# One pool for the output stage and the feed-forward weights of a hybrid decoder layer

## The chip, the cores and the metric

The kernel runs on one core of a Trainium2 chip. The metric is the device time of one execution in microseconds (us). TensorE (PE) multiplies matrices and loads their weights in a separate step (PEld), VectorE (DVE) and ScalarE (ACT) do elementwise work and conversions, GpSimd (POOL) does elementwise work on on-chip memory, and SyncE (SP) issues the transfers. Each engine takes its instructions in the order of its own queue.

## The reference

The reference computes one decoder layer on 1024 tokens of width 1024, with 16 learned tokens in front.

```python
u = rmsnorm(h, attn_norm_w[l])
proj = u @ w_in[l]
...
o_gdn = gated_deltanet_group(...)            # 4 heads of 128, chunked delta rule
o_fox = forgetting_attention_group(...)      # 8 heads of 64, softmax with a forget-gate bias
h = h + jnp.concatenate([o_gdn, o_fox], axis=-1) @ w_out[l]
h = h + swiglu(rmsnorm(h, ffn_norm_w[l]), w_gate[l], w_up[l], w_down[l])
...
h = rmsnorm(h, final_norm_w)
return h[:, N_META:]

def swiglu(x, w_gate, w_up, w_down):
    return (jax.nn.silu(x @ w_gate) * (x @ w_up)) @ w_down
```

The feed-forward width is 2816. All values are float32.

## The kernel before

Every float32 product is made of three matmuls on rounded halves: an operand is split into hi (a cast on ACT) and lo (a subtraction on DVE), and hi*hi, hi*lo and lo*hi are summed. The function split does one such split, load_w loads raw weights and splits them into a tile pair of the pool wsp, wout_block does so for one 512-column half of w_out.

The stages up to the attention are not touched. In the attention TensorE runs by an order that a planner (PeOrder, od) writes out; w_out's product with the delta-rule heads (wout_gdn, one unit per column half nb and row tile tt of 128 tokens, twelve matmuls of 512 columns) fills its gaps. There are 16 units, and the last RES = 6 are left over for the time after the attention.

Then comes the output stage. Row tiles are taken in ORDER = (0, 4, 1, 5, 2, 6, 3, 7). For each:

- prep_load loads the attention's result and its normalisers into a tile `of` (POOL adds two halves, L1101; ACT copies 1/sum, L1102).
- prep_pe transposes the normalisers on TensorE (rbt, L1111), multiplies on DVE (L1112) and splits the result into oh and ol (L160, L161).
- load_h fetches the residual (tile hst).
- out_fox(tt, nb) adds w_out's product with the attention heads for one column half: twelve matmuls (wof, L191 to L193), an add on DVE (L1176), and after the second half norm2: the square on ACT (L1044), the power on POOL (L207), the scaling xn on DVE (L1046).
- u_blocks transposes xn (u2t, L1192) and makes the operands of the feed-forward stage on DVE, ACT and POOL (L1197 to L1218).

The feed-forward stage multiplies 2 x 2 blocks with seven instead of eight products, p1 to p7 (a Strassen-Winograd scheme). For each of NF = 11 passes j and each of gate and up (m = "g", "u") w_ops loads two raw tiles, builds sums of their blocks on DVE, and splits each of the seven operands when its turn in ORD comes. block3 does twelve matmuls for one product (L1264), ffn_evict takes it out of the accumulator, down_sums prepares w_down's blocks on POOL (L1274 to L1277). The units of a pass run p1, p6, p2, p7, p5, p4, p3, each for gate and up; in the first pass p1 and p2 are prepared early and run first.

TensorE's order is the program's order in these stages (manual_schedule). The other engines' and SP's order comes from a scheduler that goes by its own time estimates; issue_after only holds an instruction behind another on the same queue. A tile's first write waits until the tile that had the place before it is done with; a pool opened with reuse_waits="tile" waits for the overlapping tiles alone, any other pool for all that lay there. In the kernel before, the first-pass tiles are placed like this:

```python
woc.close()
wrc.close()
f1[0] = f1c.enter_context(tc.tile_pool(name="f1", bufs=1, side="right", reuse_waits="tile"))
```

So the output stage's pool (wo1) and the weight pools (wraw, wsp) end, and the feed-forward weights get a new pool f1 in their place.

Of the kernel before, what the change touches and what calls it, by code (L numbers as in the profile page):

```python
# [95 lines left out]
def tile_hymba_layer(ctx, tc, x, meta, attn_norm_w, w_in, conv_w, a_log, dt_bias, gdn_norm_w,  # L96
# [57 lines left out]
    wraw = wrc.enter_context(tc.tile_pool(name="wraw", bufs=2, side="right"))  # L154
    wsp = wrc.enter_context(tc.tile_pool(name="wsp", bufs=4, side="right"))
# [8 lines left out]
    def load_w(parts, name):  # L164
# [9 lines left out]
        hi = wsp.tile([P, WMAX], F32R, tag="whi", name=f"whi_{name}")  # L174
        lo = wsp.tile([P, WMAX], F32R, tag="wlo", name=f"wlo_{name}")
# [879 lines left out]
    def wout_block(k0, nb):  # L1055
        ws = ([], [])
        for i in range(2):
            hl = load_w([(wout_w(k0 + 2 * i, nb), 1024)], f"wo{k0}_{nb}{i}")
# [23 lines left out]
    od.fill = wout_gdn_all(tiles[:len(tiles) - RES])  # L1082
# [7 lines left out]
    wo2 = woc.enter_context(tc.tile_pool(name="wo1", bufs=1, side="right", reuse_waits="tile"))  # L1090
    turn, ofs, pre_u = {}, {}, {}
# [14 lines left out]
    def prep_pe(tt):  # L1106
        of = ofs[tt]
        oh, ol = (wo_tile(t, [P, 4, P], 2, tt, F32R) for t in ("oh", "ol"))
# [13 lines left out]
    for tag in ("of_0", "of_1", "oh_0", "ol_0", "oh_1", "ol_1", "hst_0", "xn2_0", "hst_1", "xn2_1"):  # L1122
        big = tag[:2] in ("hs", "xn")
        wo2.tile([P, D] if big else [P, 8 if tag[1] == "f" else 4, P], F32R if tag[1] in "hl" else F32, tag=tag,
                 name=f"lay_{tag}")
    nwb2 = wo2.tile([P, D], F32, name="nwb2")
    od.fill = wout_gdn_all(tiles[len(tiles) - RES:])
    prep_load(ORDER[0])
    with tc.issue_after(last_o[0].ins):
        nc.sync.dma_start(nwb2, ffn_norm_w[0].partition_broadcast(P))  # L1130
    prep_load(ORDER[1])
# [7 lines left out]
    peo.close()  # L1139
    rot[0] = 1  # L1140
    wo0c.close()
    alc.close()
    ogc.close()
    akc.close()
    gplc.close()
    H, NF = 512, NFF // 2
    ORD = ("p1", "p6", "p2", "p7", "p5", "p4", "p3")
    CH = ((0, 4), (4, 4), (8, 3))

    def chunked(nm, ps):  # L1150
        t = {(p, f0): dram.tile([P, n, H], F32, name=f"{nm}_{p}{f0}") for p in ps for f0, n in CH}
        return t, {(p, f0 + i): t[p, f0][:, i] for p in ps for f0, n in CH for i in range(n)}

    ao_c, ao_d = chunked("ao", ORD)
    wt_c, wt_d = chunked("wt", ("p5", "p6", "p7", "p4"))
    w_g_v = w_gate.rearrange("(k p) n -> p k n", p=P)
    w_u_v = w_up.rearrange("(k p) n -> p k n", p=P)

    uoc, pfc, f1c = ExitStack(), ExitStack(), ExitStack()
    uop = uoc.enter_context(tc.tile_pool(name="uop", bufs=1, reuse_waits="tile"))  # L1160
    uop.tile([P, 120], F32, name="upad")

    def blk(c, p, nm=None):
        return uop.tile([P, 4, H], F32R, tag=f"u{c}_{p}", name=nm or f"u{c}_{p}")

    uo = {p: tuple(blk(c, p) for c in "hl") for p in ORD}
    pfp = pfc.enter_context(tc.tile_pool(name="pf", bufs=1, reuse_waits="tile"))
# [14 lines left out]

    tops = {}

    def u_blocks(tt):
# [14 lines left out]
        if tt < 4:  # L1200
            br = [wo_tile(f"br{g}", [P, 4, P], 1, tt) for g in range(2)]
# [5 lines left out]
        b12, t2, t3 = (wo_tile(f"ub{i}", [P, 4, P], 1, tt) for i in range(3))  # L1207
# [12 lines left out]
    f1, raw_dma = [None], {}  # L1220
# [7 lines left out]
    def pf_tile(i, nm, dt=F32R):  # L1228
        return pfp.tile([P, D], F32R, tag=f"pf{i}", name=nm)
# [3 lines left out]

    def w_ops(v, j, m):
        r0, r1 = (f1[0].tile([P, D], F32, tag="raw", bufs=4, name=f"raw_{m}{j}_{i}") for i in range(2))
        for r, f in ((r0, j), (r1, j + NF)):
            raw_dma[m, j] = w_raw(r, v, f)
        a11, a12, a21, a22 = r0[:, :H], r0[:, H:], r1[:, :H], r1[:, H:]
        s2, s3, s4 = (f1[0].tile([P, H], F32, tag=f"ws{i}", bufs=2, name=f"ws{i}_{m}{j}") for i in range(3))
        if not j:  # L1240
            V.tensor_tensor(s3, a21, a22, op=ALU.add)
# [3 lines left out]
            V.tensor_tensor(s4, a12, s2, op=ALU.subtract)  # L1245
            V.tensor_tensor(a11, a11, a21, op=ALU.subtract)
            srcs = (None, s2, None, a11, s3, a22, s4)
        else:
            V.tensor_tensor(s3, a11, a21, op=ALU.subtract)
            V.tensor_tensor(a21, a21, a22, op=ALU.add)  # L1250
            V.tensor_tensor(s2, a21, a11, op=ALU.subtract)
            V.tensor_tensor(s4, a12, s2, op=ALU.subtract)
# [294 lines left out]
```

## Time and profile before

| | |
|---|---|
| median of 3 runs | 1349.8 us (1348.13 to 1351.02) |
| profiled execution | 1348.91 us, span of its profile 1347.2 us |
| DVE, ACT, POOL busy in the span | 894.9, 553.9, 426.1 us |
| output stage in the trace | from 612 us (last value product of the attention) to about 727 us |
| feed-forward, first two weight matrices | about 700 to 1129 us |
| w_down and final norm | about 1129 us to the end |

Times in views of the trace count from the start of the span. Busy time of an engine is the time in which it executed something; a wait is put down to the instruction that released it. Weight loads (PEld) overlap with matmuls. "clock" is the share of full speed that was granted to TensorE.

### The profile page before, as it was taken

The page shows a single profiled execution, that of the slowest core. Times are in us where ns is not written, and L with a number is a line of the kernel's source. Part 1 is how long each engine was busy: PE and PEld are TensorE (multiplying, and loading weights), DVE is VectorE, ACT ScalarE, POOL GpSimd, SP SyncE. Part 2 cuts the span into 40 slices and gives each one's busy share as a digit, 9 for nine tenths or more (in the row PEclk, how much of TensorE's full clock was granted, in tenths as well). Part 3 has the DMA queues.
Part 4 walks back from the last instruction along what each step waited for, and adds up shares of the span by engine and source line. Part 5 has one row for each costly group of instructions (what it writes and reads, how often), then busy time and mean ns, then how long its engine had stood idle before and what let it go on. Part 6 is the DMA issues. An engine that isn't in the chain of part 4 may idle for free.

```text
span 1347.2 us, 20241 instructions
## 1 busy us (share of the span) xinstructions
PE 1305.9 (97%) x7442; PEld 1137.6 (84%) x7442; DVE 894.9 (66%) x1509; ACT 553.9 (41%) x926; POOL 426.1 (32%) x414
## 2 busy tenths in 40 slices
PE   8999999999999999999898999999999999999997
PEld 7999998899999877887676888888888888888886
DVE  6465778758446578894879667766777765455644
ACT  6443444322223476883553233333332343333332
POOL 3111114211012255661333545543444343010301
PEclk9999999999999999999988999999999999999999
DMA  8121555684589698846556554454444446954523
GB/s 292 54 84 55 146 163 157 182 236 132 164 267 301 168 286 223 222 115 199 175 154 192 180 177 136 156 168 161 163 158 164 156 176 232 410 205 173 208 71 125
DMA packets 196922, 242.12 MB, mean 180 GB/s; under 512 B 19024, under 2 KB 146888, under 8 KB 193112
## 3 DMA queue, kind: packets, MB, share of 16 engines
q1 hardware_dynamic: 196824, 240.84, 56.4%
q8 instruction: 58, 0.95, 0.3%
q14 instruction: 40, 0.33, 0.1%
HBM read 161.62 MB, written 79.18 MB: 179 GB/s over the span
## 4 chain that ended last, share of the span: by engine, by line
PE 79%; DMA 8%; DVE 7%; issue 2%; SPq 2%; POOL 1%; ACT 1%; POOLq 0%; DVEq 0%; ACTq 0%
PE xp L1433 9%; PE yp L1433 7%; PE ub L1264 5%; PE gd L1264 4%; PE ud L1264 4%; PE ga L1264 4%; PE ua L1264 4%; PE gb L1264 4%; PE pj_fk L201 3%; PE pj_fq L201 3%; PE ue L1264 2%; PE ge L1264 2%; PE pt L967 2%; PE po L988 1%; DMA of<-o_d 1%
## 5 line engine op out<-in xcount | busy, mean ns | idle before, releaser
L161 DVE TENSOR_TENSOR al_p<-ra_p,ah_p 128x2048 fp32r<-128x2048 f32 (+1 forms) x21 | 47.1, 2243 | 92.7 <-ACT ah_p L160 92.7
L920 POOL TENSOR_TENSOR bi<-ccol,cr 128x144 f32<-128x144 f32 (+7 forms) x60 | 69.7, 1167 | 54.5 <-DVE sm L936 32.3
L160 ACT CAST ah_p<-ra_p 128x2048 fp32r<-128x2048 f32 (+1 forms) x21 | 37.1, 1767 | 105.2 <-PE xp L1433 48.5
L1433 PE MATMUL xp<-wh_p,ah_p 128*128 128x512 f32 (+1 forms) x187 | 70.5, 377 | 0.7 <-DVE hs L1460 0.7
L1433 PE MATMUL xp<-wl_p,ah_p 128*128 128x512 f32 (+1 forms) x187 | 70.4, 376 | 0.0
L1433 PE MATMUL xp<-wh_p,al_p 128*128 128x512 f32 (+1 forms) x187 | 70.4, 376 | 0.0
L1274 POOL TENSOR_TENSOR dt<-raw_d,raw_d 128x512 f32<-128x512 f32 x11 | 17.7, 1607 | 141.3 <-issue 95.1
L160 ACT CAST wh_u_p<-raw_u 128x512 fp32r<-128x512 f32 x42 | 26.1, 622 | 77.6 <-PE gd L1264 40.1
L941 ACT ACTIVATE pr<-pr,sm 128x144 f32<-128x144 f32 (+3 forms) x64 | 50.5, 789 | 11.0 <-DVE sm L936 9.9
L161 DVE TENSOR_TENSOR pl<-pt,ph 128x512 fp32r<-128x512 f32 (+1 forms) x96 | 51.9, 552 | 3.9 <-ACT ph L160 3.0
L160 ACT CAST ph<-pt 128x512 fp32r<-128x512 f32 (+1 forms) x96 | 45.3, 473 | 19.4 <-PE pt L967 18.4
L160 ACT CAST wh_g_p<-raw_g 128x512 fp32r<-128x512 f32 x42 | 26.1, 622 | 65.3 <-PE ub L1264 37.9
L1433 PE MATMUL yp<-wh_p,ah_p 128*128 128x512 f32 x132 | 51.3, 389 | 0.0
L1433 PE MATMUL yp<-wl_p,ah_p 128*128 128x512 f32 x132 | 51.3, 389 | 0.0
L1433 PE MATMUL yp<-wh_p,al_p 128*128 128x512 f32 x132 | 51.3, 389 | 0.0
L161 DVE TENSOR_TENSOR wl_p<-rw_p,wh_p 128x2048 fp32r<-128x2048 f32 (+1 forms) x21 | 46.9, 2235 | 3.4 <-ACT wh_p L160 3.4
L967 PE MATMUL pt<-ident,pr 128*128 128x128 f32 x288 | 48.1, 276 | 0.0
L160 ACT CAST wh_u_p<-ws_u 128x512 fp32r<-128x512 f32 x33 | 20.5, 622 | 56.5 <-PE gb L1264 21.3
L933 PE MATMUL sc<-kk,sa 128*128 128x144 f32 (+6 forms) x112 | 40.6, 363 | 3.2 <-DVE sm L936 2.0
L161 DVE TENSOR_TENSOR wl_u_p<-raw_u,wh_u_p 128x512 fp32r<-128x512 f32 x42 | 33.8, 804 | 13.6 <-ACT wh_u_p L160 13.6
L1433 PEld LDWEIGHTS xp<-wh_p,ah_p 128*128 128x128 f32 x187 | 35.2, 188 | 7.4 <-DVE hs L1460 0.9
L936 DVE CUSTOM_DVE_ANT_0 pr<-sc,bi 128x144 f32<-128x144 f32 (+3 forms) x64 | 31.3, 492 | 14.2 <-POOL bi L922 5.3
(621 smaller groups left out, 4574.6 us busy)
## 6 DMA issues: line engine op xcount, KB each, us to landing
ra_p<-ao_p SPq DMA_DIRECT2D x14, 1024.0 KB, 4.9
raw_g<-in_w_gate_dram SPq DMA_DIRECT2D x23, 512.0 KB, 4.8
raw_u<-in_w_up_dram SPq DMA_DIRECT2D x23, 512.0 KB, 4.1
raw_d<-in_w_down_dram SPq DMA_DIRECT2D x22, 512.0 KB, 6.1
wt_p<-raw_d SPq DMA_DIRECT2D x33, 256.0 KB, 2.0
rw_p<-wt_p SPq DMA_DIRECT2D x8, 1024.0 KB
kk<-k_d SPq DMA_DIRECT2D x14, 520.0 KB, 9.1
rw_p<-in_w_down_dram SPq DMA_DIRECT2D x6, 1024.0 KB, 4.9
```

The lines of the kernel that those rows point to most:

```text
L160: cast = nc.scalar.copy(dst_hi, src)
L161: tail[0] = (cast, nc.vector.tensor_sub(dst_lo, src, dst_hi.bitcast(F32)))
L201: nc.tensor.matmul(dst, a, b, start=first, stop=last)
L920: nc.gpsimd.tensor_tensor(bi[:, :n], ccol[:, h, j:j + 1].broadcast_to([P, n]), cr[:, :n], op=ALU.subtract)
L933: nc.tensor.matmul(sc[:, :b - a], sa[:, q0:q0 + P], kk[:, 0, a:b], start=True, stop=False)
L936: V.tensor_tensor_reduce(out=pr[:, a:b], in0=sc[:, :b - a], in1=bi[:, a:b], scale=1.0, scalar=3e38 if i == 0 else sm[:, i - 1:i], op0=ALU. ...
L941: nc.scalar.activation(pr[:, :n], pr[:, :n], AF.Exp, bias=sm[:, np_ - 1:np_], scale=-1.0, accum_out=rsum[:, h, j:j + 1])
L967: nc.tensor.transpose(pt[:rows_k, P * j:P * j + P], pts[j][0][:, c0:c0 + rows_k], ident)
L988: nc.tensor.matmul(po[:, q], vt[:, kt], pl[:, q], start=False, stop=(kt == nk - 1))
L1264: nc.tensor.matmul(dst, a[:, c], b[:, k], start=(first and k == 0 and i == 0), stop=(k == 3 and i == 2), skip_group_check=not first)
L1274: G.tensor_tensor(t3, b22, b12, op=ALU.subtract)
L1433: nc.tensor.matmul(dst[:, n_], a[:, f, c], b[:, f, n_], start=(first and i == 0 and n == 0), stop=(i == NF - 1 and n == 2), skip_group_che ...
```

## The change

It does four things. The pool f1 goes away: the feed-forward weights, raw tiles and sums take turns in the tiles of the output stage's pool (RING for seven split operands, RAWS for raw tiles) and of wraw and wsp. The second column half of w_out for the attention heads is split into four tiles of a pool pf, no longer into wsp. The six left-over products are placed one or two at a time between the preparation and the products of the first row tiles, and out_fox for row tiles 0 and 4 moves ahead of the feed-forward stage's start. The sums for p6 of the first pass stand ahead of u_blocks of the last row tile.

```diff
-    wraw = wrc.enter_context(tc.tile_pool(name="wraw", bufs=2, side="right"))
-    wsp = wrc.enter_context(tc.tile_pool(name="wsp", bufs=4, side="right"))
+    wraw = wrc.enter_context(tc.tile_pool(name="wraw", bufs=2, side="right", reuse_waits="tile"))
+    wsp = wrc.enter_context(tc.tile_pool(name="wsp", bufs=4, side="right", reuse_waits="tile"))
...
-    od.fill = wout_gdn_all(tiles[:len(tiles) - RES])
+    res = [(1, tt) for tt in ORDER if tt not in (0, 1)][:RES]
+    od.fill = wout_gdn_all([x for x in tiles if x not in res])
...
+    H = 512
+    RING = ("ohl_0", "ohl_1", "nwb", "hst_1", "xn2_1", "br", "ub")
+    RAWS = {"g": ("hst_0", "of_0"), "u": ("xn2_0", "of_1")}
...
-    for tag in ("of_0", "of_1", "oh_0", "ol_0", "oh_1", "ol_1", "hst_0", "xn2_0", "hst_1", "xn2_1"):
...
-    od.fill = wout_gdn_all(tiles[len(tiles) - RES:])
     prep_load(ORDER[0])
...
-    wfs = [wout_block(4, 0)]
-    for _ in range(38):
-        od.step_fill()
-    casts = [prep_pe(ORDER[0])]
-    while od.step_fill():
-        pass
-    casts.append(prep_pe(ORDER[1]))
...
+    for tag in RING + ("hst_0", "of_0", "xn2_0", "of_1"):
+        wo2.tile([P, D], F32, tag=tag, name=f"lay_{tag}")
...
+    pfp = woc.enter_context(tc.tile_pool(name="pf", bufs=1, side="right", reuse_waits="tile"))
+    wfs = [wout_block(4, 0), wout_block(4, 1, lambda i: [pf_tile(2 * i + c, f"wf{c}_{i}") for c in range(2)])]
+    res_units(2)
+    casts = [prep_pe(ORDER[0])]
+    load_h(ORDER[0])
+    res_units(1)
+    out_fox(ORDER[0], 0)
+    prep_load(ORDER[2])
+    out_fox(ORDER[0], 1)
+    casts.append(prep_pe(ORDER[1]))
+    load_h(ORDER[1])
+    res_units(1)
+    out_fox(ORDER[1], 0)
+    prep_load(ORDER[3])
+    prep_pe(ORDER[2])
+    load_h(ORDER[2])
+    out_fox(ORDER[1], 1)
+    res_units(len(res))
+    prep_pe(ORDER[3])
+    load_h(ORDER[3])
...
     def w_split(m, j, p, src, hl=None):
-        hi, lo = hl or (f1[0].tile([P, H], F32R, tag=f"w{c}", bufs=7, name=f"w{c}_{m}{j}_{p}") for c in "hl")
-        split(hi, lo, src)
-        wops[m, j][p] = (hi, lo)
+        if hl is None:
+            t = wo2.tile([P, 2, H], F32R, tag=RING[ring[0] % len(RING)], name=f"w_{m}{j}_{p}")
+            ring[0] += 1
+            hl = t[:, 0], t[:, 1]
+        split(*hl, src)
+        wops[m, j][p] = hl
...
     def w_ops(v, j, m):
-        r0, r1 = (f1[0].tile([P, D], F32, tag="raw", bufs=4, name=f"raw_{m}{j}_{i}") for i in range(2))
-        for r, f in ((r0, j), (r1, j + NF)):
-            raw_dma[m, j] = w_raw(r, v, f)
+        r0 = wo2.tile([P, D], F32, tag=RAWS[m][0], name=f"raw_{m}{j}_0") if j else raw0[m]
+        r1 = wo2.tile([P, D], F32, tag=RAWS[m][1], name=f"raw_{m}{j}_1")
+        if j:
+            w_raw(r0, v, j)
+        raw_dma[m, j] = w_raw(r1, v, j + NF)
...
-        s2, s3, s4 = (f1[0].tile([P, H], F32, tag=f"ws{i}", bufs=2, name=f"ws{i}_{m}{j}") for i in range(3))
         if not j:
+            t = wo2.tile([P, 2, H], F32, tag=RAWS[m][0], name=f"ws_{m}0")
+            s2, s3 = t[:, 0], t[:, 1]
...
-            V.tensor_tensor(s4, a12, s2, op=ALU.subtract)
...
         else:
+            s2, s3 = halves(wraw, "raw", f"ws_{m}{j}")
...
+            if p == "p2":
+                V.tensor_tensor(a12, a12, s2, op=ALU.subtract)
...
-        t3 = f1[0].tile([P, H], F32, tag="dt3", bufs=1, name=f"dt3_{j}")
+        t3 = sbs["u", j]["t"]
...
-            with tc.issue_after(first6[m].ins) if p == "p2" and not j else nullcontext():
-                ffn_evict(m, j, p, ffn_bank(m, j, p))
+            ffn_evict(m, j, p, ffn_bank(m, j, p))
...
-        with tc.issue_after(last_o[0].ins):
-            for tt in ORDER[:2]:
-                load_h(tt)
-        with tc.issue_after(casts[0].ins):
-            wfs.append(wout_block(4, 1))
         for i, tt in enumerate(ORDER):
+            if i < 2:
+                continue
             out_fox(tt, 0)
-            if i >= 2:
-                u_blocks(ORDER[i - 2])
+            u_blocks(ORDER[i - 2])
...
-                    r = wraw.tile([P, WMAX], F32, tag="raw", name=f"raw_{m}")[:, :D]
-                    w_raw(r, v, 0)
-                    hi, lo = (pf_tile(2 * "gu".index(m) + i, f"w{c}_{m}0") for i, c in enumerate("hl"))
+                    raw0[m] = wraw.tile([P, WMAX], F32, tag="raw", name=f"raw_{m}")[:, :D]
+                    w_raw(raw0[m], v, 0)
+                    hi, lo = (wsp.tile([P, WMAX], F32R, tag=f"w{c}", name=f"w{c}_{m}0") for c in ("hi", "lo"))
...
-        u_blocks(ORDER[7])
-        woc.close()
-        wrc.close()
-        f1[0] = f1c.enter_context(tc.tile_pool(name="f1", bufs=1, side="right", reuse_waits="tile"))
...
         for m in "gu":
             next(gens[m])
             first6[m] = tail[0][1]
+        u_blocks(ORDER[7])
```

The tiles of the feed-forward sums (x, y, z, w, two passes in flight) become halves of wsp's tiles. In the output stage oh and ol become the two halves of one tile ohl, the two tiles br0 and br1 become halves of br, and b12 and t2 halves of ub.

More of the change, by code (lines that the diff above doesn't have):

```diff
@@ L173, in load_w @@
             o += m
-        hi = wsp.tile([P, WMAX], F32R, tag="whi", name=f"whi_{name}")
-        lo = wsp.tile([P, WMAX], F32R, tag="wlo", name=f"wlo_{name}")
+        hi, lo = hl or (wsp.tile([P, WMAX], F32R, tag=f"w{c}", name=f"w{c}_{name}") for c in ("hi", "lo"))
         split(hi[:, :n], lo[:, :n], raw[:, :n])
@@ L1200, in u_blocks @@
         if tt < 4:
-            br = [wo_tile(f"br{g}", [P, 4, P], 1, tt) for g in range(2)]
+            br2 = wo_tile("br", [P, 2, 4, P], 1, tt, slot="br")
+            br = br2[:, 0], br2[:, 1]
             for g, p in enumerate(("p1", "p2")):
```

114 lines of the change are left out of this document (56 added, 58 removed).

## The prediction

> **What bounds the kernel now.** First the page's busy shares, then busy time in stretches cut at the stage's own events, then what TensorE (PE) waited for in the output stage (total, times, longest). A stretch's columns are span, busy time of PE, its weight loads, DVE, ACT and POOL, granted clock, DMA. Line numbers are the old kernel's.
>
> ```profile
> span 1347.2 us, 20241 instructions
> PE 1305.9 (97%) x7442; PEld 1137.6 (84%) x7442; DVE 894.9 (66%) x1509; ACT 553.9 (41%) x926; POOL 426.1 (32%) x414
> ...
> core 0: us, PE busy (x) PEld busy (x) DVE busy (x) ACT busy (x) POOL busy (x), PEclk, DMA share, GB/s
> 612.26:645.62 33.36, 30.80 (x138) 24.09 (x139) 15.44 (x23) 11.43 (x18) 6.13 (x5) 1.00 0.72 215
> 645.62:667.54 21.92, 21.06 (x109) 16.78 (x108) 16.64 (x25) 11.47 (x22) 7.61 (x7) 1.00 0.68 215
> 667.54:681.42 13.88, 9.97 (x36) 7.90 (x37) 11.00 (x14) 6.86 (x13) 6.40 (x7) 0.75 0.36 115
> 681.42:699.98 18.56, 15.82 (x76) 13.01 (x75) 16.57 (x24) 11.10 (x21) 8.19 (x7) 0.91 0.36 114
> 699.98:726.89 26.91, 21.37 (x81) 16.26 (x81) 22.57 (x26) 11.11 (x21) 12.68 (x9) 0.87 0.58 165
> 726.89:1110.00 383.11, 383.11 (x1691) 317.22 (x1691) 272.26 (x336) 123.30 (x203) 173.21 (x110) 1.00 0.50 166
> ...
> PE wof L193 <- DVE ol L161: 3.9, 1, 3.9
> PE u2t L1192 <- DVE xn L1046: 2.7, 1, 2.7
> PE ub L1264 <- DVE wl_u_p L161: 2.6, 1, 2.6
> PE gb L1264 <- ACT wh_g_p L160: 2.4, 1, 2.4
> PE rbt L1111 <- ACT of L1102: 1.3, 1, 1.3
> PE wof L192 <- DVE wlo_wo L161: 0.8, 1, 0.8
> ```
>
> PE is busy 97% of the span, so only PE's gaps and slow stretches can be won. The last stretch is the feed-forward loop: 383.11 us, all of it busy, clock 1.00, nothing to win. The five stretches before it are the output stage, from the last value product of the attention to the end of the first half of the p6 blocks. Call them A to E. Span minus PE busy gives their idle time: A 33.36 - 30.80 = 2.56, B 0.86, C 3.91, D 2.74, E 5.54, together 15.6 us. The waits name the owners: A waits for the weight split of w_out's second half (L160, L161) and for L1102's copy; C for ol (L161); D for xn (L1046); E for the splits wh_g_p, wl_g_p, wl_u_p.
>
> The clock column is below 1.00 in C, D and E, and that is a second loss, read from the chain of waits by the pace of single pieces:
>
> ```profile
> 648.42 0.87 PE u2t L1192 x8
> 697.05 0.43 PE wof L191
> 699.28 0.23 PE wof L191
> 786.73 2.72 PE ga L1264 x12
> ```
>
> These rows are start, time and instruction. A 512-column matmul takes 0.23 us at full clock and 0.43 us behind the gap in D. At full clock twelve of them are 2.72 us in the loop (2.8 for one out_fox, by the same 0.23) and eight transposes 0.87 us. C holds two out_fox (12 matmuls each), one u_blocks and one prep_pe (about 0.5): 5.6 + 0.9 + 0.5 = 7.0 us of work, and took 9.97 busy: 3.0 lost. D holds four out_fox and three u_blocks: 13.8, took 15.8: 2.0 lost. E holds six blocks and one u_blocks: 17.2, took 21.4: 4.2 lost. So the stage gives away 15.6 + 9.2 = 24.8 us, and that is the ceiling: A 2.6, B 0.9, C 6.9, D 4.7, E 9.7.
>
> **Part 1: second half of w_out in tiles of its own, left-over products spread.** The six left-over products (twelve 0.23 us matmuls each) keep their number. PE's new order is two products, prep_pe(0), one product, out_fox(0,0), out_fox(0,1), prep_pe(4), one, out_fox(4,0), prep_pe(1), out_fox(4,1), two, prep_pe(5). PE's sum is the same; what changes is what each step may have to wait for.
>
> ```profile
> 524.37 0.37 SPq L172 DMA_DIRECT2D raw_wo<-in_w_out_dram  x1
> 616.21 0.37 SPq L1100 DMA_DIRECT2D of<-o_d  x1
> ...
> 622.71 1.30 POOL L1101 TENSOR_TENSOR of<-of 128x512 f32<-128x512 f32 x1 [7.07 <-DMA of<-o_d]
> ...
> 612.00:620.00 8.00, 8.00 (x37) 6.56 (x37) 1.43 (x3) 1.21 (x2) 1.29 (x1) 1.00 0.83 220
> ...
> 624.03 0.62 ACT L1102 COPY of<-rinv 128x512 f32<-128x512 f32 x1 [7.75 <-POOL of L1101]
> 624.56 0.62 ACT L160 CAST oh<-of 128x512 fp32r<-128x512 f32 x1
> 632.05 1.99 ACT L160 CAST whi_wo<-raw_wo 128x1024 fp32r<-128x1024 f32 x2
> ...
> 621.42 0.68 DVE L1112 TENSOR_TENSOR of<-rbt,of 128x512 f32<-128x512 f32 x1
> 633.13 1.23 DVE L161 TENSOR_TENSOR wlo_wo<-raw_wo,whi_wo 128x1024 fp32r<-128x1024 f32 x1 [2.88 <-ACT whi_wo L160]
> ```
>
> The raw weights of the second half were issued at 524.37, far ahead, but the tiles for their split are those of the left-over products' weights. So ACT casts at 632.05, once the last product is done, DVE subtracts at 633.13, and PE waits. With own tiles over dead attention memory the two casts (1.0 us each) and two subtractions (1.2 each) can run from 612 on, where DVE is busy 1.43 of 8 us and ACT 1.21. If the order puts them before 612 they sit between the attention's last steps: at most 2 x 1.2 = 2.4 us on DVE, at least nothing. I take 0.5, nearer to the free stretch.
>
> Now the chain for out_fox(0,0). From 612.26 PE does two products (5.5), the four transposes (0.5), one product (2.8), and wants oh and ol at 621.0. After the transposes, 618.3, DVE multiplies (0.68, L1112), ACT casts (0.62) and DVE subtracts (about 0.7, as L1112): 620.5 with the steps between. That fits by half a microsecond if ACT takes the cast first. Before, it did not: L1112 ended at 622.1 and the cast of oh began at 624.56, behind the copy of tile 4's rinv (L1102), itself behind the load issued at 616.21, whose sum on POOL began at 622.71. That is rival 1. Tile 4's transposes come at 626.6 in the new order and its copy ends at 624.65, so they fit. The loads for tiles 1 and 5 can start when ol(0) and ol(4) free their buffers, about 620.5 and 630. With tile 4's 6.5 us of load, 1.3 on POOL and 0.6 on ACT they are ready at 629 and 638.5, and PE asks at 632.6 and 641.4. On SP's queue these loads, four h_d loads and the first gate and up loads come earlier than now; the same bytes, covered by those 3 us. Without the cover each microsecond of lateness is one of PE. What is late next in A is ol(0), so of A's 2.6 I count 1.6, less the 0.5: **1.1**.
>
> **Part 2: stretches B, C, D.** PE's order there is untouched. What changes is the backlog.
>
> ```profile
> 669.24 2.28 DVE L1046 SCALAR_TENSOR_TENSOR xn<-hst,st_f,nwb 128x1024 f32<-128x1024 f32 x1 [0.44 <-POOL st_f L207]
> 671.44 0.68 DVE L161 TENSOR_TENSOR ol<-of,oh 128x512 fp32r<-128x512 f32 x1
> 693.14 1.28 DVE L1046 SCALAR_TENSOR_TENSOR xn<-hst,st_f,nwb 128x1024 f32<-128x1024 f32 x1
> ```
>
> In C ol stood on DVE's queue behind xn (begun 669.24, 2.28 us) and began at 671.44, and PE waited 3.9 us for it. DVE is busy 16.64 + 11.00 + 16.57 = 44.2 us in B to D, and PE's work there at full clock is 20.9 + 7.0 + 13.8 = 41.7, so DVE is as much a bound as PE. In the new order tile 4's last add and ol(5) (0.7 each) and xn(4) (1.3) fall before B; four subtractions for the first gate and up blocks (0.7 each) fall into it, since their tiles now are those of the left-over products: 44.2 - 2.7 + 2.8 = 44.3. The three stretches, now 54.4 us, go no lower than that, so the gain lies between 10.1 and, if the order on DVE clots as before, nothing. D's chain of add, square, power and xn (693.14) ahead of the last transposes keeps its order and most of its wait; C's wait for one late ol goes with a pipeline that starts two tiles further on. I take 4.7 of the 7.8 in B and C, and 1.2 of D's 4.7: **5.9**, near the middle.
>
> **Part 3: one pool, so the p6 weights come earlier.** Now all four raw tiles of the first pass are loaded only after the old pools close.
>
> ```profile
> 678.31 1.44 DVE L161 TENSOR_TENSOR ol<-of,oh 128x512 fp32r<-128x512 f32 x1
> 687.43 0.68 DVE L161 TENSOR_TENSOR ol<-of,oh 128x512 fp32r<-128x512 f32 x1
> ...
> 699.98:706.00 6.02, 6.02 (x31) 5.02 (x31) 2.22 (x4) 2.74 (x5) 1.35 (x2) 1.00 0.80 220
> ...
> 701.22 1.40 SPq L1232 DMA_DIRECT2D raw_g<-in_w_gate_dram  x2
> ...
> 711.02 1.77 DVE L1241 TENSOR_TENSOR ws_g<-raw_g 128x512 f32<-128x512 f32 x1
> 713.55 0.69 DVE L1245 TENSOR_TENSOR ws_g<-raw_g,ws_g 128x512 f32<-128x512 f32 x1
> 720.43 1.75 DVE L1246 TENSOR_TENSOR raw_u<-raw_u,raw_u 128x512 f32<-128x512 f32 x1
> ...
> 714.76 1.82 POOL L1274 TENSOR_TENSOR dt<-raw_d,raw_d 128x512 f32<-128x512 f32 x1 [2.52 <-DMA raw_d<-in_w_down_dram]
> ```
>
> The loads are issued at 701.22, just after the last out_fox; u_blocks(7) has DVE until 711.0, and the sums for p6 (L1241 on) follow it. In the new kernel the first halves are there already; the second halves go into of_0 and of_1, free after ol(3) and ol(7), 679.8 and 688.1, and land some 5 us later. The sums' tiles (hst_0, xn2_0) come free after xn(3) (694.4) and its transposes (695.8). From 699.98 to 706 DVE is busy 2.22 of 6.02 us, and six operations (two sums, one subtraction, for gate and up) need 6 x 0.69 = 4.1. PE does p1 (5.4), eight transposes and p2 (5.4), and asks for p6 at 711.8: E's idle time and slow clock go. Late next is u_blocks(7) on DVE, moved behind these six, for p6's activations; a slip of 2 us there shows. Bounds: 9.7, or nothing. I take **7.5**, nearer to the row with 3.8 us free. Two of the 512 KB loads and the wait for first6 at p2 go too: nothing, hidden under p1.
>
> The rows have a price for the other end. L1241 and L1246 take 1.77 and 1.75 us while POOL works (L1274 from 714.76 and its three successors, before them u_blocks), L1245 with POOL idle 0.69. POOL's down sums can now start right after the last out_fox, since their tiles are those of w_out's second half, and so may meet the p6 sums and u_blocks(7). [...]
>
> **Part 4: the loop.** Matmuls, seven weight tiles in flight and two sets of sums stay; down's t3 moves into a half tile, wraw and wsp wait per tile with nothing below them: nothing. The raw tiles' slots become fixed: the first half of each matrix is held until its p3 split, the thirteenth or fourteenth of 14 (a12 - s2 now goes in place), not until p2. With seven tiles that split can run when PE has done the sixth block, and its reload is wanted after the fourteenth: eight blocks x 2.72 = 21.8 us.
>
> ```profile
> DMA to landing us min/median/max: 3.6/4.3/6.8
> ```
>
> The slowest load lands after 6.8 us; cast and subtraction are 1.3. That leaves 13.7 us of cover, so I cost it at nothing; without the cover it is rival 4. After the loop the program is the same: nothing.
>
> **Sum.** 1.1 + 5.9 + 7.5 = 14.5 us off the profiled execution, 1348.9 (span 1347.2 and 1.7 around it): 1334.4. The median of the runs is 0.9 above, so 1335.3.
>
> **Rivals.** 1: ACT again takes tile 4's copy ahead of oh(0). Then out_fox(0,0) starts at 625.9 instead of 621.0, and the slow pace after such a gap costs about 2, as in D: 1335.3 + 6.9 = 1342. For it speaks 624.03 before 624.56; against it, oh(0) is now ready 3 us earlier while that load is not. 2: DVE is the bound. Each of the six operations before p6 meets one of POOL and takes 1.0 us more, E gains 3.7 instead of 9.7, B to D gain 2: 1348.9 - 1.1 - 2 - 3.7 + 0.9 = 1343. For it, the 1.75 against 0.69; against it, POOL is busy only 1.35 of the 6.02 us from 699.98. 3: the change does not do what it says: buffers come free no earlier than now, nothing moves, 1350. Against it, the rows 524.37 and 678.31 show data and buffers early. 4, slower: the reload after p3 comes so late that DVE, in order, holds the adds that free PE's accumulators. The gain of 14.5 is used up at 1.5 us in each of ten passes; at 3 us it is 1335 + 30 = 1365. Against it, 13.7 us of cover and a loop without idle PE. 5: everything is won, 24.8 us: 1325.
>
> **How the numbers follow.** Forecast 0.50, from 1328 to 1340; rival 1 0.16, rival 2 0.14, rival 3 0.06, rival 4 0.07, rival 5 0.07. The range takes in the forecast and rivals 1, 2 and 5, and leaves out 3 and 4 and what lies past the ceiling: 1325 to 1348. A difference of 0.2%, 2.7 us, is about what a measurement of this kernel tells from none. Faster 0.87, same 0.06, slower 0.07.
>
> **What would show it.** Right: casts of whi_wo near 613 and no wait of L191 or L192 on them; oh(0) on ACT before the second rinv copy; the wait on ol near 672 under 2 us and the clock there near 1.00; gate and up loads at 680 to 690; p6 directly behind p2. Wrong: a gap before the first out_fox, new waits of the loop on raw_g or raw_u, PE no longer full after the first pass, or sums of 1.7 us beside POOL ahead of p6.

## The result, and the profile after

The changed kernel is slower: 1359.59 us median (1358.48 to 1361.21, 4 runs) against 1349.30 for the kernel before (4 runs beside it), a ratio of 1.0076 with a 95% interval of 1.0059 to 1.0094. That is +10 us where I had forecast -14.5.

First the busy times of the changed kernel's page. Then its stretches A to E, cut at the same events as in the prediction, and the loop from the first block of the second pass to w_down; that loop in the kernel before follows in a fence of its own.

```profile
span 1356.8 us, 20203 instructions
PE 1305.2 (96%) x7442; PEld 1132.7 (83%) x7442; DVE 882.3 (65%) x1509; ACT 550.7 (41%) x926; POOL 431.6 (32%) x414
```

```profile
611.27:642.29 31.02, 30.05 (x138) 23.78 (x138) 14.76 (x21) 10.40 (x16) 6.25 (x6) 1.00 0.90 270
642.29:663.46 21.17, 21.05 (x112) 17.11 (x110) 15.45 (x25) 12.66 (x24) 7.39 (x6) 1.00 0.53 176
663.46:672.38 8.92, 7.53 (x39) 5.54 (x38) 7.28 (x12) 4.60 (x9) 4.04 (x4) 1.00 0.55 176
672.38:693.08 20.70, 14.49 (x76) 11.45 (x74) 18.96 (x26) 12.18 (x23) 9.74 (x8) 1.00 0.47 156
693.08:719.28 26.20, 19.75 (x81) 15.27 (x80) 23.66 (x30) 11.73 (x21) 12.70 (x9) 0.93 0.41 141
741.04:1139.49 398.45, 386.18 (x1681) 315.43 (x1680) 257.23 (x319) 118.33 (x197) 176.42 (x109) 1.00 0.48 156
```

```profile
748.49:1129.29 380.80, 380.80 (x1682) 315.31 (x1681) 267.95 (x321) 124.51 (x199) 166.22 (x107) 1.00 0.49 165
```

The time is lost in one place. The loop takes 398.45 us instead of 380.80: 17.65 lost. For 12.27 of these PE is idle (398.45 - 386.18); the other 5.4 are matmuls that took longer in the passes with a wait. Stretches A to E take 108.0 us instead of 114.6 (612.26 to 726.89): 6.6 won. The stage also begins 1.0 us earlier and the last part is 0.6 shorter; together 17.65 - 6.6 - 1.6 = 9.4, and the spans differ by 9.6.

Within the stage A went from 33.4 to 31.0, B from 21.9 to 21.2, C from 13.9 to 8.9. D went up from 18.6 to 20.7, and E only from 26.9 to 26.2. Now the waits of TensorE (PE), and then one pass of the loop in the timeline, rows of SP's queue, DVE and PE:

```profile
PE gd L1299 <- DVE gzw L1342: 12.2, 8, 2.8
PE u2t L1215 <- DVE xn L1045: 5.5, 3, 3.3
PE wof L192 <- DVE ohl L161: 3.8, 3, 2.9
PE ga L1299 <- DVE ul_p L1221: 3.3, 1, 3.3
```

```profile
817.20 0.39 PE L1299 MATMUL ga<-uh_p,w_g_p 128*128 128x512 f32 x1
...
834.35 2.22 SPq L1314 DMA_DIRECT2D wt_p<-raw_d  x2
836.66 0.39 SPq L1257 DMA_DIRECT2D raw_g<-in_w_gate_dram  x1
...
840.80 0.38 SPq L1257 DMA_DIRECT2D raw_g<-in_w_gate_dram  x1
...
849.99 0.69 DVE L1283 TENSOR_TENSOR ws_g<-raw_g,raw_g 128x512 f32<-128x512 f32 x1 [10.13 <-DMA raw_g<-in_w_gate_dram]
850.71 0.69 DVE L161 TENSOR_TENSOR w_g_p<-raw_g,w_g_p 128x512 fp32r<-128x512 f32 x1
851.32 0.68 DVE L1284 TENSOR_TENSOR raw_g<-raw_g 128x512 f32<-128x512 f32 x1
851.92 0.68 DVE L1342 TENSOR_TENSOR gzw<-gd,gxy 128x512 f32<-128x512 f32 x1
...
852.76 0.47 PE L1299 MATMUL gd<-uh_p,w_g_p 128*128 128x512 f32 x1 [2.75 <-DVE gzw L1342]
...
858.57 0.39 PE L1299 MATMUL ga<-uh_p,w_g_p 128*128 128x512 f32 x1
```

Read it from the bottom. The next pass starts at 858.57, 41.4 us after the last one. PE stood still for 2.75 us, for the add that takes the p5 block out of its accumulator. That add came at 851.92, because on DVE's queue three steps of the *next* pass stood ahead of it, and the first of them waited 10.13 us for raw_g. The two halves of raw_g were issued 19.5 and 23.6 us into the pass (836.66 and 840.80 less 817.20), behind stores of w_down's sums (834.35). In the kernel before, from the third of these passes on, both gate loads of a pass went out 39 to 42 us ahead of it, that is before the pass in front of it began. Here is a second gate load of the kernel before, and the first matmul of its pass:

```profile
823.44 0.38 SPq L1232 DMA_DIRECT2D raw_g<-in_w_gate_dram  x1
...
862.73 0.39 PE L1264 MATMUL ga<-uh_p,wh_g_p 128*128 128x512 f32 x1
```

This is rival 4, with a second queue in it that I had not counted.

### The profile page after: what moved, and what is told of

Its sections match the earlier page's. It is cut to its first block, busy times and chain, and to the rows that moved or that the text cites. A ratio compares the mean times of both kernels' runs of the same rounds, so it can differ in the third digit from the quotient of the medians.

```text
span 1356.8 us, 20203 instructions
## 1 busy us (share of the span) xinstructions
PE 1305.2 (96%) x7442; PEld 1132.7 (83%) x7442; DVE 882.3 (65%) x1509; ACT 550.7 (41%) x926; POOL 431.6 (32%) x414
## 4 chain that ended last, share of the span: by engine, by line
PE 68%; DMA 13%; DVE 9%; issue 4%; POOL 3%; SPq 2%; ACT 1%; POOLq 0%; DVEq 0%; ACTq 0%
PE xp L1452 8%; PE yp L1452 7%; DMA raw_g<-in_w_gate_dram 4%; PE gb L1299 4%; PE ua L1299 3%; PE ga L1299 3%; PE ub L1299 3%; PE pj_fk L200 3%; PE pj_fq L200 3%; PE gd L1299 3%; PE ud L1299 3%; PE pt L966 2%; PE wog L200 2%; PE po L987 1%; PE pj_k L191 1%
## 5 line engine op out<-in xcount | busy, mean ns | idle before, releaser
L161 DVE TENSOR_TENSOR al_p<-ra_p,ah_p 128x2048 fp32r<-128x2048 f32 (+1 forms) x21 | 46.9, 2233 | 94.4 <-ACT ah_p L160 94.4
L160 ACT CAST w_g_p<-raw_g 128x512 fp32r<-128x512 f32 x53 | 32.8, 620 | 142.3 <-DMA raw_g<-in_w_gate_dram 79.4
L1299 PE MATMUL gd<-uh_p,w_g_p 128*128 128x512 f32 x176 | 59.6, 400 | 12.2 <-DVE gzw L1342 12.2
L161 DVE TENSOR_TENSOR w_g_p<-raw_g,w_g_p 128x512 fp32r<-128x512 f32 x53 | 56.8, 1071 | 4.2 <-ACT w_g_p L160 3.9
L1299 PE MATMUL ud<-uh_p,w_u_p 128*128 128x512 f32 x176 | 58.5, 393 | 0.1
L161 DVE TENSOR_TENSOR w_u_p<-raw_u,w_u_p 128x512 fp32r<-128x512 f32 x53 | 45.7, 863 | 19.0 <-ACT w_u_p L160 19.0
L1299 PE MATMUL gb<-uh_p,w_g_p 128*128 128x512 f32 x176 | 57.8, 389 | 0.0
L1299 PE MATMUL ub<-uh_p,w_u_p 128*128 128x512 f32 x176 | 57.8, 389 | 0.0
L160 ACT CAST ph<-pt 128x512 fp32r<-128x512 f32 (+1 forms) x96 | 45.2, 472 | 21.2 <-PE pt L966 20.2
L1347 POOL TENSOR_TENSOR gxy<-gxy,uxy 128x512 f32<-128x512 f32 x22 | 35.0, 1593 | 56.7 <-DVE uxy L1342 40.5
L1299 PE MATMUL ua<-uh_p,w_u_p 128*128 128x512 f32 x160 | 52.5, 389 | 0.0
L1299 PE MATMUL ga<-uh_p,w_g_p 128*128 128x512 f32 x160 | 52.5, 389 | 0.0
```

Source lines behind the costliest of these rows:

```text
L160: cast = nc.scalar.copy(dst_hi, src)
L161: tail[0] = (cast, nc.vector.tensor_sub(dst_lo, src, dst_hi.bitcast(F32)))
L1299: nc.tensor.matmul(dst, a[:, c], b[:, k], start=(first and k == 0 and i == 0), stop=(k == 3 and i == 2), skip_group_check=not first)
L1347: G.tensor_tensor(gs[d], gs[d], us[d], op=ALU.mult)
```

## Experiments on the loop

"Theory 1" is that the raw tiles' new places and DVE's order make the wait; its rivals are named in the expectations. Each loop below is cut at the same two events.

**The loads ahead of the stores (e3).** The next pass's raw tiles are loaded before down_sums in the program, and the stores of the sums are held behind the first half's load:

```diff
+            if j + 1 < NF:
+                for m, v in (("g", w_g_v), ("u", w_u_v)):
+                    raws_of[m, j + 1] = w_load(v, j + 1, m)
             down_sums(j)
...
+        with tc.issue_after(raw_dma["u", j + 1, 0].ins) if j + 1 < NF else nullcontext():
             for p, t in (("p7", t3), ("p5", b12), ("p6", b22), ("p4", b21)):
                 nc.sync.dma_start(wt_d[p, j], t)
```

> The changed kernel with the raw loads of the next pass ahead of the stores of w_down's sums in SP's queue, so that no load stands behind a store that waits for POOL (in the changed kernel the load of raw_g for the pass at 858.73 was issued at 836.66, behind two stores that waited for POOL until 836.2, though its place was free at about 830). The order on DVE stays: the sum still stands ahead of the p5 add. Theory 1b (SP's order makes the loads late): 1343 to 1348 us. Theory 1 in its narrow form (the late release of the places and the order on DVE make it, SP adds little): 1355 to 1360 us.

1342.87 us, 0.9948 of before (0.9933 to 0.9963). The loop's stretch, and a pass of it in the timeline:

```profile
743.00:1123.80 380.80, 380.80 (x1681) 315.31 (x1680) 250.25 (x320) 122.18 (x198) 174.62 (x110) 1.00 0.50 165
```

```profile
819.16 0.39 PE L1305 MATMUL ga<-uh_p,w_g_p 128*128 128x512 f32 x1
...
832.15 0.38 SPq L1257 DMA_DIRECT2D raw_g<-in_w_gate_dram  x1
...
837.26 0.61 SPq L1257 DMA_DIRECT2D raw_g<-in_w_gate_dram  x1
```

All 17.65 us are back, with DVE's order as it was. The gate loads go out 13.0 and 18.1 us into the pass, 6 us earlier than in the changed kernel. Theory 1b holds: SP's queue made them late.

**The places of before (e4).** The tiles that come free first go to the next gate, and the last sum has its own tile:

```diff
+        tags = RAWS[m] if j % 2 or not j else (RAWS["g"][m == "u"], RAWS["u"][m == "u"])
...
+            s4 = wo2.tile([P, H], F32, tag="ws4", bufs=2, name=f"ws4_{m}{j}")
+            V.tensor_tensor(s4, a12, s2, op=ALU.subtract)
```

> The changed kernel with the places of the raw tiles taken as in the kernel before: the two tiles that are free first (after p2 of gate and of up) go to the next pass's gate, and the last sum has a tile of its own, so that no raw tile is held until p3. Everything else of the change stays, the shared half tiles and the ring of split operands too. Theory 1: gate's loads are issued some 15 us earlier in the pass, the waits of PE for the p5 add go, 1342 us (1339 to 1346). Theory 2 also expects 1342 us here. Theory 3: 1357 to 1362 us.

1343.27 us, 0.9952 (0.9937 to 0.9968); the loop takes 380.80 us again, so the loss is the loads' lateness, by whatever it is cured. The shared half tiles and the ring stayed, so theory 3, in which these make DVE wait, is out.

**t3 in its own tile (e5).** One line decided SP's order:

```diff
-        t3 = sbs["u", j]["t"]
+        t3 = wo2.tile([P, H], F32, tag="dt3", bufs=1, name=f"dt3_{j}")
```

> The changed kernel with one line altered: t3, the first sum of w_down's blocks, gets a tile of its own again instead of a half of the u sums' tile. Fixed places of the raw tiles, sums in place, shared half tiles and the order in which the program states things stay. In the order of SP's queue this puts the stores of w_down's sums behind the raw loads of the next pass, as in the kernel before; with the shared half tile they stand ahead of them. Theory 1b (late loads, because they stand on SP behind stores that wait for POOL): the loop takes 381 us again instead of 398.5, 1342 to 1345 us. Theory 1c (the fixed places still cost what they cost in the kernel before, 4.3 us): 1346 to 1349 us. If the half tile is not the cause: 1357 to 1361 us.

1349.09 us, 1.0003 (0.9988 to 1.0017). The loop's stretch, and SP's queue in the timeline:

```profile
747.05:1130.77 383.72, 383.07 (x1681) 314.61 (x1680) 275.41 (x319) 118.37 (x198) 163.72 (x106) 1.00 0.49 159
```

```profile
842.95 0.38 SPq L1257 DMA_DIRECT2D raw_g<-in_w_gate_dram  x1
...
849.47 0.34 SPq L1314 DMA_DIRECT2D wt_p<-dt  x1
```

The stores stand behind the loads again, and 14.7 of the loop's 17.65 us are back. (The whole kernel gained 10 us, from 1.0076 to 1.0003 of the time before; in this profile D and E take 50.0 us, in that of the changed kernel 46.9.) With the half tile POOL's down sums, and with them the stores, had slid by part of a pass to a place in front of the next loads; that they wait there for the u sums in the other half is argued, not shown. 2.9 us stay: theory 1c.

**The held places alone, in the kernel before (e2).**

```diff
-        r0, r1 = (f1[0].tile([P, D], F32, tag="raw", bufs=4, name=f"raw_{m}{j}_{i}") for i in range(2))
+        r0, r1 = (f1[0].tile([P, D], F32, tag=f"raw{m}{i}", name=f"raw_{m}{j}_{i}") for i in range(2))
...
+            if p == "p2":
+                V.tensor_tensor(a12, a12, s2, op=ALU.subtract)
```

> The kernel before with two things of the changed kernel's loop and nothing else of the change: each raw tile has a fixed place that the same tile of the next pass takes again, and the last sum is built in place in the raw tile, which holds it until p3. Its output stage, its pools and its tiles for the products of gate and up stay. Theory 1 (the late hold of the raw tiles makes the loss): a pass takes 40 to 41 us instead of 38.1, PE waits for the p5 add, and the time is 1349 + 17.7 = 1367 us (1360 to 1370). Theory 3 (the shared half tiles, the ring of split operands or the halves of the old weight tiles make it): no change, 1348 to 1351 us.

1353.94 us, 1.0031 (1.0016 to 1.0046); the loop takes 385.57 us, 4.8 more. Neither theory had this: theory 1 in the form that I had gave 17.7, theory 3 nothing. The held places are worth 3 to 5 us, and only with SP's order do they make 17.65.

**DVE's sums behind the adds (e1).**

```diff
+            with tc.issue_after(ev["u", j - 1, "p5"].ins):
                 V.tensor_tensor(s3, a11, a21, op=ALU.subtract)
...
+                with tc.issue_after(ev["u", j - 1, "p5"].ins) if j and p == "p1" else nullcontext():
                     w_split(m, j, p, src)
```

> The changed kernel with one thing altered in the loop: the weight sums of the next pass and the lo split of its p1 operand are held on DVE behind the p5 add of u. Raw tiles, sums in place, transfers and their order on SP stay as in the changed kernel. Theory 1 (the raw loads come late, and DVE, which takes its queue in order, stands before a sum or a split that needs them while the p5 add that frees PE's accumulator stands behind it): the waits of PE for the p5 add of g, 11.7 us over the loop, go, a pass takes 38.1 us again instead of 40 to 41, and the time is that of the changed kernel less the 17.7 us that its loop lost, 1342 us (1339 to 1346). Theory 2 (the weights reach PE too late for PE's own sake, since the loads are as late and as bunched as before): the waits move from the add to the split weights of p1, and the time stays at 1355 to 1360 us. Theory 3 (DVE has too much to do, or the shared half tiles make it wait): 1357 to 1362 us.

1364.78 us, 1.0115 (1.0081 to 1.0148): no faster, and rather slower than the changed kernel (1.0059 to 1.0094). The loop's stretch, and PE's waits in it:

```profile
741.28:1142.08 400.80, 388.01 (x1681) 317.63 (x1680) 288.07 (x323) 116.95 (x199) 174.55 (x111) 0.99 0.48 158
```

```profile
PE gb L1301 <- DVE w_g_p L161: 7.2, 5, 1.7
...
PE gd L1301 <- DVE gzw L1344: 5.2, 1, 5.2
```

In the first nine of the ten passes the wait for the add is gone, and in the last five one for the weights of p6 stands there: theory 2. The nine lost 10.8 us together, against 16.8 in the changed kernel. The last pass alone lost 9.2: PE waited 5.2 us for its p5 add, which stood on DVE's queue behind a first split of w_down's operands (al_p), and the matmuls behind that wait took 0.63 us instead of 0.39. The first four passes take 38.08 us, but in each the second gate load goes out closer to the pass that uses it, 18.5 us ahead at first and 11 after five passes; as I read it, sums that run later free the raw tiles later. After the fifth pass (38.45 us) they take 40 to 42 us, and the last 47.3. Order alone won 6 us of nine passes' loss and did not pay for late data.

**All together.** By the time in a pass at which the second gate load goes out, and what that pass takes beyond 38.08 us (both from the issue rows and the first matmuls of nine passes of each kernel): 17.9 to 18.6 us and nothing in e3; 17.9 to 19.7 and at most 0.9 in e5; 18.0 to 20.7 and at most 1.7 in e2; in the changed kernel 18.7 and 20.4 and nothing in the first two passes, then 22.6 to 23.9 and 1.0 to 4.1. So up to 18.6 us no pass lost anything that counts, from 18.7 to 20.7 some lost up to 1.7 and others nothing, and from 22.6 on every pass lost 1.0 or more: an edge that is not sharp. By the prediction's own count the load would have gone out at 38.1 - 21.8 = 16.3.

## Experiments on the output stage

In the changed kernel DVE works without a gap from 689.79 to 702.2, and this is its order:

```profile
690.88 1.78 DVE L1275 TENSOR_TENSOR ws_g<-raw_g 128x512 f32<-128x512 f32 x1
692.58 1.77 DVE L1275 TENSOR_TENSOR ws_u<-raw_u 128x512 f32<-128x512 f32 x1
694.27 0.68 DVE L1221 TENSOR_TENSOR ul_p<-u2t,uh_p 128x512 fp32r<-128x512 f32 x1
...
698.47 0.68 DVE L1291 TENSOR_TENSOR raw_g<-raw_g,ws_g 128x512 f32<-128x512 f32 x1
...
699.68 0.68 DVE L1137 TENSOR_TENSOR hst<-wof,hst 128x512 f32<-128x512 f32 x1
...
703.41 2.32 DVE L1045 SCALAR_TENSOR_TENSOR xn<-hst,st_f,nwb 128x1024 f32<-128x1024 f32 x1 [0.67 <-POOL st_f L206]
```

The sums for p6 stand ahead of operands (ul_p) that PE waits 3.3 us for, and the last sum in place (L1291), wanted at p3, ahead of the last residual add, ready since 693.

**Sums held back (e6, e56).** On top of e3, and of e5:

```diff
+            with tc.issue_after(ev["add"].ins):        # out_fox(7, 1)
                 V.tensor_tensor(s3, a21, a22, op=ALU.add)
...
+            with tc.issue_after(ev["put"].ins):        # last operand of u_blocks(7)
                 V.tensor_tensor(a11, a11, a21, op=ALU.subtract)
...
             if p == "p2":
+                with nullcontext() if j else tc.issue_after(ev["put"].ins):
                     V.tensor_tensor(a12, a12, s2, op=ALU.subtract)
```

> The changed kernel with the next pass's loads ahead of the stores of w_down's sums (1342.9 us by itself) and with a second thing: in the output stage the sums for p6 of the first pass are held on DVE behind the last residual add of row tile 7, and its two sums in place behind the last operand of the last row tile. Theory A (what the third and fourth row tiles' stretches did not win is DVE's order: sums that PE needs late stand ahead of adds and operands that it needs soon): the waits of PE for ul_p (3.3 and 1.2 us) and for xn of row tile 7 (1.9 us) go for the most part, 3 to 6 us, 1337 to 1340 us. Theory B (DVE has no time left there, beside POOL): the waits go elsewhere, 1342 to 1344 us.

> The changed kernel with two things: t3 in a tile of its own, and the first-pass sums held on DVE behind the last residual add and the last operand of row tile 7, the loads in the order that the program had. If both theories hold (late loads through SP's order in the loop, DVE's order in the output stage), the time is that of the run with t3 apart less 3 to 6 us: 1337 to 1341 us. If only the loop's holds: 1342 to 1345 us.

e6: 1343.57 us, 0.9956 (0.9935 to 0.9976), no gain that can be told from e3 alone. e56: 1344.11, 0.9973 (0.9957 to 0.9990), 5.0 us less than its base e5 as measured, so within theory A's 3 to 6; but the two intervals still overlap, and by itself e56 is no faster than e3. In e6 the wait moved:

```profile
PE gb L1309 <- DVE gxy L1353: 4.9, 1, 4.9
```

**More held back (e9).** The last sum in place and the splits of p5, p4 and p3 stand back too, behind the p6 add of u:

```diff
+            hold = not j and p in ("p2", "p5", "p4", "p3")
+            with tc.issue_after(ev["u", 0, "p6"].ins) if hold else nullcontext():
                 if p not in wops[m, j]:
                     w_split(m, j, p, src)
                 if p == "p2":
                     V.tensor_tensor(a12, a12, s2, op=ALU.subtract)
```

> The kernel with the loads first, with the first-pass sums held as in the run with the order, and beyond that the last sum in place and the splits of p5, p4 and p3 of the first pass held on DVE behind the p6 add of u. In the run with the order alone PE waited 4.9 us for the p6 add of g (DVE at 722.87), which stood behind two such sums of 1.77 and 0.68 us, a first sum of 1.78 us and four splits. Theory A' (the order is right, but more has to stand back): that wait goes and the stage is 3 to 5 us shorter than its base, 1338 to 1340 us. Theory B (DVE has no time left between 689 and 720 us, whatever the order): within 2 us of its base.

1340.26 us, 0.9924 (0.9912 to 0.9936), and its base e3 on the same chip 1345.05, 0.9962 (0.9949 to 0.9975). A second run of e9 gave 1339.16, 0.9925 (0.9905 to 0.9945). Stretch E and a wait:

```profile
696.13:717.84 21.71, 18.07 (x81) 14.05 (x80) 20.86 (x25) 11.57 (x21) 12.76 (x9) 1.00 0.22 84
```

```profile
PE gb L1310 <- DVE gxy L1354: 1.6, 1, 1.6
```

E falls to 21.7 us, from 26.2 in the changed kernel and 24.1 in its base, and the wait that was 4.9 us in e6 to 1.6; D and E together fall from 47.0 in the base to 43.4: theory A'.

**POOL off DVE's back (e8).** On e3, POOL's three steps of u_blocks go to DVE for row tiles 6 and 7.

```diff
+        late = V if tt in (6, 7) else G
+        late.tensor_tensor(t4, t4, t2, op=ALU.subtract)
...
+        put("p5", t1, late)
+        put("p4", t4, late)
```

> The kernel with the loads first, with POOL's three steps of u_blocks (one subtraction, two lo parts) moved to DVE for row tiles 6 and 7. In the changed kernel nine DVE steps between 689 and 717 us took 1.17 to 2.32 us where the same steps elsewhere take 0.68 (1.28 for xn), 7.3 us more together, and POOL worked beside them; the six steps would cost DVE 6 x 0.68 = 4.1 us. Theory B1 (DVE is the bound of that stretch and POOL beside it makes its steps longer): the long steps go, 3 us less at most, 1339 to 1342 us against 1343 for its base. Theory B2 (it is the bound and POOL has no part in the length of the steps): 4 us more. Theory C (DVE's work there is not on the path): no change.

1344.34 us, 0.9960 (0.9948 to 0.9972): no change against 1345.05. But not for the reason of theory C, as the timeline and the waits show:

```profile
701.37 4.63 POOL L1316 TENSOR_TENSOR uzt<-raw_d,raw_d 128x512 f32<-128x512 f32 x1 [9.83 <-DMA raw_d<-in_w_down_dram]
...
707.31 0.55 POOL L206 TENSOR_TENSOR st_f<-st_f,mhalf 128x1 f32<-128x1 f32 x1
...
707.89 2.27 DVE L1045 SCALAR_TENSOR_TENSOR xn<-hst,st_f,nwb 128x1024 f32<-128x1024 f32 x1 [2.94 <-POOL st_f L206]
```

```profile
PE u2t L1215 <- DVE xn L1045: 8.9, 3, 6.4
```

Every 512-column step of DVE from 693 to 705 took 0.65 to 0.70 us (theory B1 as to the steps, not as to the time), but POOL then began w_down's first sum earlier, took 4.63 us for it beside the busy DVE (1.7 on average in the loop of the changed kernel), and the power of the last norm stood behind it: PE waited 6.4 us. The gain was spent in a new wait.

**The two left-over causes (e10, e11, e12).** On e9: a third place for the residual tile (e10); the edit of e8 with POOL's first w_down sum held behind the last power (e11); both (e12).

```diff
-        ht = wo_tile("hst", [P, D], 2, tt)
+        ht = wo_tile("hst", [P, D], 3, tt)
...
+        with nullcontext() if j else tc.issue_after(pw[0].ins):
             G.tensor_tensor(t3, b22, b12, op=ALU.subtract)
```

> Its base with a third place for the residual tile hst, so that the load for a row tile no longer waits for xn of the row tile two before it. In its base's chain of waits such a load stands at 675.85 for 4.71 us, released by xn, and after it come an add, xn of the same row tile and the lo part ohl, for which TensorE waited 2.9 us. Theory H (that load is on the path of the stretch before the first feed-forward block): the stretch falls from 21.7 us to 18 or 19, the wait for ohl goes, 3 us less. Theory C (it is hidden; the stretch is bound by DVE's work): no change.

> Its base with POOL's three steps of u_blocks moved to DVE for row tiles 6 and 7, and with POOL's first sum for w_down held behind the power of row tile 7's norm. In the run that moved the steps alone, the long DVE steps went, but POOL took 4.63 us for that sum while DVE worked back to back, the power stood behind it, and TensorE waited 6.4 us for xn. Theory P (with the power free of it, DVE's shorter steps are worth their 3 us): 1 to 3 us less than its base. Theory N (what the long steps cost and what the six moved steps cost balance): within 1 us of its base.

> Its base with both edits. If theories H and P both hold: 4 to 6 us less than the base, 1334 to 1336 us where the kernel before has 1349.7. If H alone: 3 us less; if neither: no change.

Beside e9's 1339.16 us: e10 1338.38, 0.9916 (0.9896 to 0.9936); e11 1338.06, 0.9919 (0.9899 to 0.9940); e12 1336.76, 0.9906 (0.9887 to 0.9926). Their gains of 0.8, 1.1 and 2.4 us are smaller than the intervals; only the direction agrees, and e11 does not decide between P and N. In e11 E falls close to its work of 17.2 us, but D, in the first row, takes 22.99 us against 20.54 in the second run of e9, at a clock of 0.85:

```profile
675.23:698.22 22.99, 17.44 (x76) 13.85 (x74) 20.40 (x31) 12.18 (x23) 4.89 (x5) 0.85 0.44 140
698.22:716.68 18.46, 18.05 (x81) 14.05 (x80) 17.36 (x25) 11.86 (x21) 7.70 (x5) 1.00 0.26 97
```

So by these two profiles most of what E won went into D. In e10 the residual load is gone from the chain of waits, but PE still waits 2.6 us for ohl, a wait that theory H had go. D has 19.4 us there, against 21.7 and 20.5 in the two runs of e9, which differ by as much among themselves: theory H is not shown. e12 is the best of all, 12.6 us faster than before. What else holds D is left open.

**The spread undone (e7 on e6, e7b on e3).** The edit is the same in both:

```diff
-    res_units(2)
+    res_units(3)
     casts = [prep_pe(ORDER[0])]
     load_h(ORDER[0])
-    res_units(1)
+    res_units(3)
+    casts.append(prep_pe(ORDER[1]))
+    load_h(ORDER[1])
     out_fox(ORDER[0], 0)
...
-    casts.append(prep_pe(ORDER[1]))
-    load_h(ORDER[1])
-    res_units(1)
...
-    res_units(len(res))
```

> The kernel of the run with the loads first and the sums held, with the spread of the left-over products undone: three of them before the first row tile's preparation, three before the second's, and only then the products of the attention heads. My prediction gave the spread 1.1 us; the first stretch of the changed kernel was 2.4 us shorter than before. If the spread carries that stretch's gain, this is 2 to 3 us longer than the kernel it is made from; by the prediction's figure 1 us; if the gain is in the early residual loads and w_out halves, no longer.

> The kernel with the loads first, with the spread of the left-over products undone, and nothing else. The same edit on the kernel with the held sums gave a stage of 133.42 us against 132.75, and a median that was 4.3 us longer but with intervals that overlap. If the spread carries the 2.4 us that the first stretch won: 2 to 3 us longer than its base; by the prediction's figure 1.1 us longer; if it carries nothing: no change.

e7: 1347.85 us, 0.9984 (0.9961 to 1.0006). e7b: 1345.70, 0.9970 (0.9958 to 0.9982) against its base's 1345.05. Both intervals overlap those of their bases. Stretches A to C in one, in e7b:

```profile
615.58:679.18 63.60, 60.09 (x282) 48.62 (x282) 38.93 (x57) 27.78 (x48) 18.36 (x16) 0.95 0.67 215
```

That is 63.6 us against 61.9 in e3's second run, and in e7 63.1 against 61.9 in e6. So by two pairs of profiles the spread is worth 1.2 to 1.7 us; the medians cannot tell it.

## Why the prediction was wrong

The step that failed is Part 4's cost of nothing for the loop. Even without the loop's loss the forecast was too large: parts 1 to 3 came to 6.6 of 14.5 us.

**Part 4, the loop, 0 forecast, 17.65 measured.** This step turned the sign. "down's t3 moves into a half tile", put at nothing, was its dearest clause: 14.7 us (e5). I costed the tile by its size and did not ask which step would now wait for it (POOL's sum), what stands behind that on SP (the stores), and what behind those (the raw loads). "13.7 us of cover" failed as well. I counted from the reload to the moment PE needs p1. But the first reader of raw_g is a sum on DVE, in front of the p5 add, and PE needs that add for p3 g, two blocks (5.4 us) before the pass ends. The landing time changed too: six loads now go out within 5 us, and the slowest load of these weights landed after 9.6 us, not 6.8:

```profile
DMA to landing us min/median/max: 3.7/5.6/9.6
```

Rival 4 named the mechanism, and 1.5 us in each of ten passes as the point from which it decides; it was 1.8.

**Part 1, A, 1.1 forecast, 2.3 measured.** Right in mechanism. oh(0) was ready in time (PE waited 0.6 us for it), so rival 1 did not come, and no wait for the split of w_out's second half is left. The spread explains 1.2 to 1.7 of what A to C won.

**Part 2, B and C 4.7, D 1.2 forecast; 0.8 + 5.0 and -2.1 measured.** B and C were right: the clock in C is 1.00 instead of 0.75, and the 3.9 us wait for ol is gone. D was wrong: a wait for the lo part came back in it (2.9 us for ohl), beside 3.3 for xn. What would remove it is open.

**Part 3, E, 7.5 forecast, 0.7 measured.** The data came early, as said; the step that failed is "nearer to the row with 3.8 us free". That row was the old kernel's DVE from 699.98 to 706. Because the data were early, the new sums did not go there; the scheduler placed them from 690.88 on, ahead of work that PE was waiting for. It was part rival 2, which had 1343 for DVE as the bound: two sums of 1.77 us beside POOL, as priced. With order and POOL mended E came to 18.46 us (e11), 8.5 less than before, but D then took 4.4 more than before. D and E together won 4.0 us there and 4.6 at best (e12), where 8.7 were forecast for the two; that the 7.5 could be had without paying in D is not shown.

## What to carry to other kernels

When a tile is shared to save space, write down who writes it next and follow every in-order queue behind that writer to its end: here POOL, SP, the load, DVE, PE. Count the cover of a load to its first reader's place in that reader's queue, not to the engine that needs the result. Data that arrive earlier can make a stage slower, if the scheduler then runs their steps ahead of ones that someone waits for; hold them back by name.

## What the runs showed of the hardware

A slow spell followed the same wait in one run and not in the other. In the two runs of e9 PE waited 2.88 us at the same place; behind it a matmul took 0.63 us in the first and 0.40 in the second, and PE was busy for 16.07 and 14.50 us in D, at a clock of 0.92 and 1.00, with the same work. The first run, and then the second:

```profile
684.84 0.71 PE L192 MATMUL wof<-whi_wo,ohl 128*128 128x512 f32 x1 [2.88 <-DVE ohl L161]
685.35 0.63 PE L190 MATMUL wof<-whi_wo,ohl 128*128 128x512 f32 x1
```

```profile
674.43:696.13 21.70, 16.07 (x75) 12.59 (x74) 18.48 (x26) 12.19 (x23) 9.76 (x8) 0.92 0.46 147
```

```profile
682.28 0.50 PE L192 MATMUL wof<-whi_wo,ohl 128*128 128x512 f32 x1 [2.88 <-DVE ohl L161]
682.62 0.40 PE L190 MATMUL wof<-whi_wo,ohl 128*128 128x512 f32 x1
```

```profile
672.01:692.55 20.54, 14.50 (x76) 11.46 (x74) 18.35 (x26) 12.18 (x23) 9.74 (x8) 1.00 0.49 157
```

So two profiles of one kernel differ in this stretch by 1.2 us in span and 1.6 us in PE's busy time, without a cause in the kernel. In the loop of the changed kernel, too, matmuls took 0.63 us behind a wait of 2.21 us (at 1014.18), but 0.39 to 0.40 behind one of 2.75 us (at 852.76). So in these runs the length of the wait alone did not decide whether a slow spell followed; what does is not shown.

In e8 steps of POOL and DVE that ran at the same time had very different lengths. A sum on POOL took 4.63 us (from 701.37), against 1.7 on average in the loop of the changed kernel, while five DVE steps from 701.78 on took 0.70 us each. And xn on DVE took 2.27 us (from 707.89) with a POOL sum of 1.26 us beside it (from 707.82), against 1.28 at 691.58, where POOL was idle. What decides which of the two takes longer is not shown.
